# A DiT block with 32 experts on one core: front projections in three float32r passes, a shared stream ring, and the last two experts in column groups

## The chip, the core and the metric

The kernel runs on one core of one Trainium2 chip. The metric is device time in microseconds of one execution: the median of the runs. One more execution was recorded by the hardware profiler, and all rows below are from it. The engines are TensorE (PE in the rows, with its weight loads as PEld), VectorE (DVE), ScalarE (ACT), GpSimd (POOL) and SyncE (SP), whose queue issues the weight transfers.

## What is computed

One block of a diffusion transformer, in fp32, on 256 tokens of width 1024 with 256 context tokens: two kinds of attention with gates, then a mixture of 32 experts, four of them for each token.

```
h  = modulate(rms_norm(x), sh1, sc1);  hc = modulate(rms_norm(ctx), csh1, csc1)
p  = h @ w_in                            # keys, values, queries, two gates: 512 + 1024 + 2048 columns
k, v also from hc                        # context keys and values: the first 512 columns
y_a = global_attn(rope(norm(q_a)), k_a, v_a);  y_b = window_attn(rope(q_b), k_b, v_b, sink)
x  = x + g1 * ((sigmoid(g_a) * (y_a @ w_br_a) + sigmoid(g_b) * (y_b @ w_br_b)) @ w_o)
h2 = modulate(rms_norm(x), sh2, sc2)
combine = softmax of the 4 largest of (h2 @ w_router + b_router), else 0
for e in range(32):
    u   = h2 @ w_e1[e] + b_e1[e]
    act = min(u_glu, 7) * sigmoid(1.702 * u_glu) * (clip(u_lin, -7, 7) + 1)
    out = out + combine[:, e] * (act @ w_e2[e] + b_e2[e])
out = rms_norm(x + g2 * out, final_g)
```

The six shifts, scales and gates (`sh1` to `g2`) are a product of `w_mod` with the conditioning vector. The weights of the 32 experts are 12 MB each and by far the most of what is read.

## The kernel before

Every engine runs its instructions in the order in which the code issues them (a manual schedule), and semaphores hold an instruction until its operands are there.

**The stream.** All large weights come in one list, `pieces`, through SyncE's queue alone. `pump()` (line 100) issues the next pieces as long as there is room. Room is a ring of seven areas of 128 x 4096 words (2 MB, `N_PAIR`), each of two halves. An expert's piece takes a whole area: its first weights `w1` are four pieces, its second weights `w2` two. The pieces of the front (queries `q`, projections `in`, modulation `mod`, branches and `w_o`) take one half. `take` gives a piece to its user, `done` gives its room back. After attention two more areas join, `xx` (the tokens' and the context's transposes till then) and `ptt` (attention's probabilities till then). So nine areas serve the experts, and nothing else limits how far ahead the stream may run.

**The front.** Tokens and context lie in `xx` as `x` and `xc`, transposed. `m0_prod` (253) computes the part of the modulation that the projections need. `q_prods` (294) makes the 64 products of the queries, `gate_half` (393) the gates in sixteen groups of eight products, `proj` (383) the 32 products of the keys, `values` (467) the 32 of the values. Each is a 128 x 128 weight against 256 columns in fp32, and the profile shows each as two weight loads and two matmuls. `modulate_c` (302, 303) scales each of the eight rows of the context on VectorE and shifts it on ScalarE, both in place. `rotate` (375 to 378) applies the rotary embedding to a query or key in four VectorE steps. The rest of the modulation is a row times `w_mod`, in 32 steps of 128 x 1024: `mod_v` (351) on VectorE alone, or `mod_p` (357) on GpSimd with its sum on ScalarE, `mod_a` (364). Attention runs in steps of `scores` (517), `turn` (551) and `weigh` (567, 572), with the last gates and modulation steps between them. Then come the merge, `w_o` (723), the norm and the router.

**The experts.** For each pair of experts 64 slots each are gathered (830). `gemm1` (860) multiplies by `w1`, the activation is four steps (from 871), `act_turn` transposes its result, `gemm2` (897) multiplies by `w2`, and a product with the slots' matrix (918) adds the result to the tokens in `ACC`.

**The end.** The last two experts take another path. Their pieces are `l1` and `l2`: quarters and halves of columns, each in two transfers with short rows (line 130 for `w1`, line 124 for `w2`). `half1` (994) and `act_half` make the last expert's activation in two halves of columns, `half2` (1133) the second product in two halves, each followed by its scatter (1149, and 1017 for expert 30). In the middle stands a branch on the number of tokens that overflowed their expert's slots: every engine loads the count (1040) and compares (1041), and the code for overflowing tokens, which doesn't run with these inputs, lies behind it. The last lines scale by the final norm and store four blocks (1167).

## Time and profile before

| | us |
|---|---|
| median of 3 runs | 1210.23 (1209.86 to 1211.34) |
| profiled execution, its own time | 1209.79 |
| its span in the trace | 1208.0 |
| TensorE busy | 1147.9 (95% of the span) |
| VectorE, ScalarE, GpSimd busy | 360.0, 138.8, 35.1 |
| moved by DMA | 458.32 MB, mean 379 GB/s |

Busy time of TensorE is modelled, and a busy TensorE isn't one at its peak. In the rows a line such as `L393 PE MATMUL mm<-xx,ring 128*128 128x256 f32 x80` reads: line 393, engine, operation, written tile and read tiles (without buffer numbers), stationary and moving shape, and the number of records that are joined in it. What stands in brackets is the idle time of the engine before it and what ended that.

### The profile page before, as it was taken

What the parts mean: (1) busy time and instruction counts of PE and PEld (TensorE: products, weight loads), DVE (VectorE), ACT (ScalarE), POOL (GpSimd) and SP (SyncE); (2) the same over time, 40 slices, a digit from 0 to 9 for tenths busy, and PEclk for the clock granted to TensorE, in tenths of its full rate; (3) what the DMA queues carried; (4) which work ended last, traced back from release to release, by engine and by line L of the source; (5) the groups of instructions that cost most, each with busy time, mean ns of one, the idle gap of its engine ahead of it and who ended that gap; (6) DMA issues with size and microseconds to landing.
All of it is one profiled execution on the core that took longest, in us unless ns stands there. A gap on an engine that the chain in (4) does not pass through costs nothing. (4 is left out here: it accounts for less than half of the span.)

```text
span 1208.0 us, 13270 instructions
## 1 busy us (share of the span) xinstructions
PE 1147.9 (95%) x5624; PEld 531.5 (44%) x5624; DVE 360.0 (30%) x765; ACT 138.8 (11%) x304; POOL 35.1 (3%) x29
## 2 busy tenths in 40 slices
PE   7999999999999999999999999999999899999986
PEld 5888666883333424343434343333333232323221
DVE  3363665332122242223222221212222222222222
ACT  2122553021000000000000000000000000000002
POOL 0231100000000000000000000000000000000000
PEclk9999999999999999999999999999999999999998
DMA  9976641978999999999999999999999999999992
GB/s 379 385 301 213 240 175 53 352 296 335 427 428 428 427 427 428 427 427 428 427 429 427 428 428 425 430 427 427 429 426 426 428 428 428 429 426 429 417 396 89
DMA packets 43279, 458.32 MB, mean 379 GB/s; under 512 B 4872, under 2 KB 5264, under 8 KB 13776
## 3 DMA queue, kind: packets, MB, share of 16 engines
q1 hardware_dynamic: 41520, 454.05, 90.3%
q10 hardware_dynamic: 1296, 2.06, 0.5%
q0 software_dynamic: 400, 1.32, 0.3%
q8 instruction: 46, 0.75, 0.2%
q14 instruction: 17, 0.14, 0.0%
HBM read 456.36 MB, written 1.05 MB: 379 GB/s over the span
## 5 line engine op out<-in xcount | busy, mean ns | idle before, releaser
L860 PE MATMUL u<-ring,t 128*64 128x512 f32 x1472 | 337.3, 599 | 19.6 <-DMA ring<-w 19.2
L860 PEld LDWEIGHTS u<-ring,t 128*64 128x64 f32 x1472 | 100.7, 137 | 214.2 <-issue 178.2
L897 PE MATMUL y<-ring,r_q 128*64 128x512 f32 x832 | 183.8, 592 | 0.0
L908 DVE TENSOR_TENSOR t<-y,r_kv 64x512 f32<-64x512 f32 x60 | 41.3, 689 | 324.8 <-PE y L897 324.4
L897 PEld LDWEIGHTS y<-ring,r_q 128*64 128x64 f32 x832 | 59.7, 137 | 118.9 <-issue 116.3
L871 DVE TENSOR_SCALAR r_q<-u 128x512 f32<-128x512 f32 x31 | 21.4, 691 | 237.0 <-PE u L860 237.0
L860 PE MATMUL u<-ptt,t 128*64 128x512 f32 x336 | 78.2, 597 | 2.5 <-DMA ptt<-w 2.2
L873 ACT ACTIVATE r_q<-r_q 128x512 f32<-128x512 f32 x31 | 19.5, 630 | 499.1 <-DVE r_q L871 499.1
L713 PE MATMUL u<-mtx,keep 128*64 128x512 f32 x256 | 62.2, 605 | 3.0 <-DVE r_q L874 3.0
L830 PEld LDWEIGHTS xg<-mtx,r_y 128*128 128x128 f32 x512 | 58.4, 192 | 12.2 <-issue 12.2
L830 PE MATMUL xg<-mtx,r_y 128*128 128x128 f32 x512 | 61.3, 278 | 0.0
L393 PE MATMUL mm<-xx,ring 128*128 128x256 f32 x256 | 59.9, 385 | 0.0
L918 PE MATMUL sp<-t,mtx 128*128 128x512 f32 x120 | 59.5, 618 | 0.0
L393 PEld LDWEIGHTS mm<-xx,ring 128*128 128x128 f32 x256 | 47.3, 190 | 12.6 <-issue 5.0
L832 DVE TENSOR_TENSOR t<-xg,modb 128x512 f32<-128x512 f32 x32 | 22.1, 691 | 88.8 <-PE xg L830 88.8
L860 PEld LDWEIGHTS u<-ptt,t 128*64 128x64 f32 x336 | 23.2, 137 | 47.6 <-issue 40.7
L860 PE MATMUL u<-xx,t 128*64 128x512 f32 x176 | 39.8, 595 | 3.8 <-DMA xx<-w 3.8
L919 DVE TENSOR_TENSOR r_t<-r_t,sp 128x512 f32<-128x512 f32 x60 | 38.4, 680 | 5.1 <-PE sp L918 5.1
L918 PEld LDWEIGHTS sp<-t,mtx 128*128 128x128 f32 x120 | 20.3, 189 | 38.9 <-issue 38.9
L897 PE MATMUL y<-xx,r_q 128*64 128x512 f32 x160 | 36.0, 592 | 0.0
L713 PEld LDWEIGHTS u<-mtx,keep 128*64 128x64 f32 x256 | 16.3, 135 | 44.5 <-issue 22.6
L887 ACT COPY r_q<-ta 128x512 f32<-128x512 f32 x31 | 18.1, 585 | 145.4 <-PE ta L884 145.4
(247 smaller groups left out, 889.9 us busy)
## 6 DMA issues: line engine op xcount, KB each, us to landing
ring<-w SPq DMA_DIRECT2D x144, 2048.0 KB, 32.2
xx<-w SPq DMA_DIRECT2D x21, 2048.0 KB, 32.4
ptt<-w SPq DMA_DIRECT2D x21, 2048.0 KB, 29.7
ring<-w_mod SPq DMA_DIRECT2D x16, 1024.0 KB, 7.2
ring<-w_in SPq DMA_DIRECT2D x10, 1024.0 KB, 9.2
ring<-w_m SPq DMA_DIRECT2D x8, 1024.0 KB, 12.6
ring<-w SPq DMA_DIRECT2D x16, 512.0 KB, 17.8
ring<-w_q SPq DMA_DIRECT2D x8, 512.0 KB, 12.3
```

The costliest lines, as they stand in the source:

```text
L393: nc.tensor.matmul(gp[0][:, 0:256], w[:, k, :], x[:, k, :], start=(k == 0), stop=(k == 7))
L713: nc.tensor.matmul(u[c0:c0 + 64, ch % 2, :], ident[:, 4 * e + ch:4 * e + ch + 1].to_broadcast([128, 64]), be1, start=True, stop=False)
L830: nc.tensor.matmul(xp[:, b, :], z[:, tb, 128 * k:128 * k + 128], S[:, tb, :], start=(tb == 0), stop=(tb == 1))
L832: nc.vector.tensor_tensor(out=XT[p][:, 4 * h:4 * h + 4, :], in0=xp, in1=sh2[:, 4 * h:4 * h + 4].unsqueeze(2).to_broadcast([128, 4, 128]), ...
L860: nc.tensor.matmul(u[c0:c0 + 64, ch % 2, :], XT[p][:, k, 64 * j:64 * j + 64], w[:, 512 * ch:512 * ch + 512], start=False, stop=(k == 7))
L871: nc.vector.tensor_scalar(out=glu.rearrange("p (b f) -> p b f", b=2), in0=v[:, :, 0, :], scalar1=LIMIT, scalar2=None, op0=ALU.min)
L873: nc.scalar.activation(out=sg, in_=glu, func=AF.Sigmoid, scale=ALPHA)
L887: nc.scalar.copy(out=aT, in_=tp)
L897: nc.tensor.matmul(y[64 * h:64 * h + 64, :], l, w[:, 512 * h:512 * h + 512], start=(k == 0), stop=(k == 7))
L908: nc.vector.tensor_tensor(out=YY[p][64 * j:64 * j + 64, 512 * h:512 * h + 512], in0=y[64 * h:64 * h + 64, :], in1=g2[64 * h:64 * h + 64, 5 ...
L918: nc.tensor.matmul(sp, t[:, tb, :], y[:, s], start=True, stop=True)
L919: nc.vector.tensor_tensor(out=ACC[0][:, tb, s], in0=ACC[0][:, tb, s], in1=sp, op=ALU.add)
```

## The change

**Three passes.** A product in fp32 becomes three products of float32r operands. Each operand is split into a high part (a copy that rounds to float32r) and a low part (the operand less its high part): high by high, high by low, low by high (`mm3`). This holds for queries, keys, values and gates. `prep` splits a block of 1024 weight columns: ScalarE copies, VectorE (GpSimd for the four blocks of keys and values) subtracts, and with the second block the piece's half of the ring is given back. Five `part` buffers of 1 MB (2048 words) hold the parts, two of them the context's (`C3`). Tokens are split row by row into `X3`. Gates are prepared one group ahead, six of them within the attention loop.

**Room.** The ring has five areas instead of seven. The parts lie in a pool of the front, which is closed after attention, and four areas (`more0` to `more3`) are made in its place; with `xx` ten areas serve the experts. Attention's probabilities lie in `xx` and in `pt1`.

**The end.** The last expert's `w1` comes in whole rows as all others (three areas and two halves). The second weights of experts 30 and 31 are packed together by columns (`w2l`): three groups of 256 columns and two of 128. `last2` multiplies both experts' activations by one group, each in its half of TensorE's columns, and `scatter2` adds one group to the tokens, squares it and multiplies it by the final gain. The branch on overflow stands behind the stores.

Small ones: three small transfers go from GpSimd's queue to ScalarE's, one `mod_v` falls away from its place, a temporary of `settle` has moved.

```diff
-N_PAIR = 7
+N_PAIR = 5
...
-    halves1()
-    at = len(pieces) - 6
-    pieces[at:at] = [("w2", (NE - 2, k), w2[NE - 2, k]) for k in range(2)]
-    halves2()
+    w1s(NE - 1, range(3))
+    pieces.extend(("l1", k, w1[NE - 1, 3, :, 2048 * k:2048 * k + 2048]) for k in range(2))
+
+    pieces.extend(("w2", (NE, c), w2l[c]) for c in range(3))
+    pieces.extend(("l2", c, w2l[3, :, 2048 * c:2048 * c + 2048]) for c in range(2))
...
+    fz = fr.enter_context(tc.tile_pool(name="fz", bufs=1))
...
+    X3 = [fz.tile([128, 8, 256], F32R, name=n) for n in ("x_hi", "x_lo")]
...
+    def lower(lo, v, hi, eng=None):
+        (eng or nc.vector).tensor_tensor(out=lo, in0=v, in1=hi.bitcast(F32), op=ALU.subtract)
+
+    def part():
+        return fz.tile([128, 2048], F32R, name="part", tag="part", bufs=5)
+
+    def prep(kind, idx, b, eng=None):
+        w = take(kind, idx)[:, 1024 * b:1024 * b + 1024]
+        hl = part()
+        hi, lo = hl[:, 0:1024], hl[:, 1024:2048]
+        nc.scalar.copy(out=hi, in_=w)
+        lower(lo, w, hi, eng)
+        cut[kind, idx, b] = (hi, lo)
+        if b or kind == "q":
+            done(kind, idx)
...
+    def mm3(ps, lt, rt, start, stop, **kw):
+        nc.tensor.matmul(ps, lt[0], rt[0], start=start, stop=False, **kw)
+        nc.tensor.matmul(ps, lt[0], rt[1], start=False, stop=False, **kw)
+        nc.tensor.matmul(ps, lt[1], rt[0], start=False, stop=stop, **kw)
...
+        nc.scalar.copy(out=X3[0][:, j, :], in_=x[:, j, :])
+        lower(X3[1][:, j, :], x[:, j, :], X3[0][:, j, :])
...
             nc.vector.scalar_tensor_tensor(out=v, in0=v, scalar=a1[:, k, 1:2], in1=rinv_c, op0=ALU.mult, op1=ALU.mult)
-            nc.scalar.activation(out=v, in_=v, func=AF.Identity, bias=mod0[:, k, 0, 1:2])
+            nc.scalar.activation(out=C3[0][:, k, :], in_=v, func=AF.Identity, bias=mod0[:, k, 0, 1:2])
+            nc.vector.scalar_tensor_tensor(out=C3[1][:, k, :], in0=v, scalar=mod0[:, k, 0, 1:2], in1=C3[0][:, k, :].bitcast(F32),
+                                           op0=ALU.add, op1=ALU.subtract)
...
-            nc.tensor.matmul(gp[0][:, 0:256], w[:, k, :], x[:, k, :], start=(k == 0), stop=(k == 7))
+            mm3(gp[0][:, 0:256], [v[:, k, :] for v in w], [v[:, k, :] for v in X3], start=(k == 0), stop=(k == 7))
...
+    prep("in", 0, 0, nc.gpsimd)
...
+    prep("in", 0, 1, nc.gpsimd)
...
     modulate_c(range(8))
...
+    prep("in", 1, 0, nc.gpsimd)
+    prep("in", 1, 1, nc.gpsimd)
...
+            if qt == 1 and u < 6:
+                gate_prep(10 + u)
             mod_v()
...
+    fr.close()
+    lz = late.enter_context(tc.tile_pool(name="lz", bufs=1, reuse_waits="tile"))
+    for i in range(4):
+        grow(lz.tile([128, 4096], F32, name=f"more{i}"))
     grow(xx)
-    grow(ptt)
-    fr.close()
...
+    def last2(c):
+        n = groups[c][1]
+        w = (take("w2", (NE, c)) if c < 3 else take("l2", c - 3)).rearrange("p (e k c) -> p e k c", e=2, k=8)
+        wl[c] = ps2.tile([128, 512], F32, name="yl", tag=("y", "tp")[c % 2])
+        for k in range(8):
+            for j, aT in enumerate((aT0, aT1)):
+                nc.tensor.matmul(wl[c][64 * j:64 * j + 64, 0:n], aT[:, k % 4, 64 * (k // 4):64 * (k // 4) + 64],
+                                 w[:, j, k, :], start=(k == 0), stop=(k == 7))
...
+            a = ACC[0][:, tb, s]
+            sp = ps2.tile([128, 512], F32, name="sp", tag=("sp", "xg")[tb], bufs=2)
+            nc.tensor.matmul(sp[:, 0:n], TT[p][:, tb, :], y_t[0][:, 1, s], start=True, stop=True)
+            nc.vector.tensor_tensor(out=a, in0=a, in1=sp[:, 0:n], op=ALU.add)
+            nc.scalar.activation(out=x_t[:, tb, s], in_=a, func=AF.Square, accum_out=fin[:, tb, c:c + 1])
+            if c < 4:
+                nc.gpsimd.tensor_tensor(out=res[:, tb, s], in0=a, in1=fg[:, s], op=ALU.mult)
...
+    for c in range(5):
+        last2(c)
+        if c:
+            scatter2(c - 1)
+    scatter2(4)
```

VectorE where the context is modulated, before (`xx` holds the context, `a_150` the scales, `qa` a query's PSUM, `sh` and `r_q` the rotation's temporary and result):

```order
L235 RECIPROCAL rinv<-rinv 128x256
L302 SCALAR_TENSOR_TENSOR xx<-xx,a_150,rinv 128x256 x8
L375 STREAM_SHUFFLE sh<-qa 128x256
L376 TENSOR_TENSOR r_q<-qa,r_t 128x256
L377 TENSOR_TENSOR sh<-sh,r_t 128x256
L378 TENSOR_TENSOR r_q<-r_q,sh 128x256
```

VectorE's first rows at the same place after, with the line numbers of the changed kernel (`part` is a part of the context; the pair repeats up to eight times):

```order
L244 RECIPROCAL rinv<-rinv 128x256
L313 SCALAR_TENSOR_TENSOR xx<-xx,a_147,rinv 128x256
L315 SCALAR_TENSOR_TENSOR part<-xx,mod_146,part 128x256
L313 SCALAR_TENSOR_TENSOR xx<-xx,a_147,rinv 128x256
L315 SCALAR_TENSOR_TENSOR part<-xx,mod_146,part 128x256
L313 SCALAR_TENSOR_TENSOR xx<-xx,a_147,rinv 128x256
L315 SCALAR_TENSOR_TENSOR part<-xx,mod_146,part 128x256
L313 SCALAR_TENSOR_TENSOR xx<-xx,a_147,rinv 128x256
L315 SCALAR_TENSOR_TENSOR part<-xx,mod_146,part 128x256
L313 SCALAR_TENSOR_TENSOR xx<-xx,a_147,rinv 128x256
```

The eight scalings, which stood in a row ahead of the rotations, now have a subtraction behind each, and the rotations stand behind all sixteen.

SyncE's queue at the end of the front, before, from the last two pieces of `w_o` to the first areas of expert weights (`w` is an expert's weights; numbers are areas):

```order
L136 DMA ring_66<-w_o 128x2048 [waits DMAHW0_49,DVE_49,Activation_49]
L136 DMA ring_67<-w_o 128x2048 [waits DMAHW1_49,PE_49]
L136 DMA xx<-w 128x4096 [waits DMAHW2_49,PE_49,Activation_49]
L136 DMA ptt<-w 128x4096 [waits DVE_49,DMAHW3_49,PE_49,Activation_49]
L136 DMA ring_68<-w 128x4096 [waits DMAHW0_49,PE_49]
L136 DMA ring_62<-w 128x4096 [waits DMAHW4_49,DMAHW1_49,PE_49]
L136 DMA ring_65<-w 128x4096 [waits DMAHW5_49,DMAHW2_49,PE_49]
L136 DMA ring_63<-w 128x4096 [waits DMAHW6_49,DMAHW3_49,PE_49]
L136 DMA ring_64<-w 128x4096 [waits DMAHW7_49,DMAHW4_49,PE_49]
L136 DMA ring_66<-w 128x4096 [waits DMAHW5_49,PE_49]
```

The same place of SyncE's queue after, where `more` are the four new areas:

```order
L118 DMA ring_64<-w_o 128x2048 [waits DMAHW0_49,Activation_49]
L118 DMA ring_65<-w_o 128x2048 [waits DMAHW1_49,DVE_49]
L118 DMA more_1960<-w 128x4096 [waits DMAHW2_49,PE_49]
L118 DMA more_1962<-w 128x4096 [waits DMAHW7_49]
L118 DMA more_1964<-w 128x4096 [waits DMAHW0_49]
L118 DMA more_1966<-w 128x4096 [waits DVE_49,DMAHW2_49,PE_49,Activation_49]
L118 DMA xx<-w 128x4096 [waits DMAHW3_49]
L118 DMA ring_66<-w 128x4096 [waits DMAHW4_49,PE_49]
L118 DMA ring_63<-w 128x4096 [waits DMAHW5_49,DVE_49,PE_49]
L118 DMA ring_62<-w 128x4096 [waits DMAHW6_49,PE_49]
L118 DMA ring_64<-w 128x4096 [waits DMAHW7_49,PE_49]
L118 DMA ring_65<-w 128x4096 [waits DMAHW3_49,DMAHW1_49,PE_49]
```

The first expert pieces went to `xx`, `ptt` and then the ring; now they go to the four areas of the closed pool, to `xx` and then the five of the ring.

SyncE's queue at the end, before, from the last expert's first weights to the load of the overflow count:

```order
L130 DMA xx<-w 128x2x512 [waits DMAHW6_49,PE_49]
L130 DMA xx<-w 128x2x512 [waits DMAHW7_49,PE_49]
L124 DMA ptt<-w 128x2x512 [waits DMAHW0_49,PE_49]
L124 DMA ptt<-w 128x2x512 [waits DMAHW1_49,PE_49]
L124 DMA ptt<-w 128x2x512 [waits DMAHW2_49,PE_49]
L124 DMA ptt<-w 128x2x512 [waits DMAHW3_49,PE_49]
L124 DMA ring_68<-w 128x2x512 [waits DMAHW4_49,PE_49]
L124 DMA ring_68<-w 128x2x512 [waits DMAHW5_49,PE_49]
L124 DMA ring_68<-w 128x2x512 [waits DMAHW6_49,PE_49]
L124 DMA ring_68<-w 128x2x512 [waits DMAHW7_49,PE_49]
L1040 TENSOR_LOAD cint [waits DVE_49]
L1040 ISA x2
```

The same place of SyncE's queue after (`w2l` is the packed second weights, `more_1964` then holds the result):

```order
L118 DMA ring_62<-w 128x2048 [waits DMAHW5_49,PE_49]
L118 DMA ring_62<-w 128x2048 [waits DMAHW6_49,PE_49]
L118 DMA ring_64<-w2l 128x4096 [waits DMAHW7_49,PE_49]
L118 DMA ring_65<-w2l 128x4096 [waits DMAHW0_49,PE_49]
L118 DMA more_1960<-w2l 128x4096 [waits DMAHW1_49,PE_49]
L118 DMA more_1962<-w2l 128x2048 [waits DMAHW2_49,PE_49]
L118 DMA more_1962<-w2l 128x2048 [waits DMAHW3_49,PE_49]
L1078 DMA out<-more_1964 128x512 [waits DMAHW4_49,Activation_49]
L1078 DMA out<-more_1964 128x512 [waits DMAHW5_49,DVE_49,Pool_49]
L1078 DMA out<-more_1964 128x512 [waits DMAHW6_49,Activation_49]
L1078 DMA out<-more_1964 128x512 [waits DMAHW7_49,DVE_49,Pool_49]
L1082 TENSOR_LOAD cint [waits DVE_49]
```

Rows of 512 words in pairs have become rows of 2048 and 4096 words, and the stores stand ahead of the load of the count and its branch, on SyncE as on the other engines.

## Rows read from the trace of the kernel before

**Rows 1.** The page's slices: GB/s moved in each of 40 equal parts of the span.
```profile
GB/s 379 385 301 213 240 175 53 352 296 335 427 428 428 427 427 428 427 427 428 427 429 427 428 428 425 430 427 427 429 426 426 428 428 428 429 426 429 417 396 89
```

**Rows 2.** Busy by stretch: us, PE, PEld, DVE, ACT, POOL, PEclk, DMA share, GB/s.
```profile
130.00:140.00 10.00, 10.00 (x65) 6.82 (x66) 6.38 (x13) 5.47 (x13) 2.39 (x1) 1.00 0.60 204
270.00:300.00 30.00, 28.52 (x152) 12.46 (x152) 7.21 (x25) 5.10 (x11) 0.00 (x0) 1.00 0.80 327
800.00:1000.00 200.00, 187.44 (x888) 69.94 (x886) 43.99 (x82) 8.41 (x15) 0.00 (x0) 1.00 1.01 427
1180.00:1185.00 5.00, 5.00 (x12) 1.47 (x12) 0.00 (x0) 0.00 (x0) 0.00 (x0) 0.66 0.49 186
1185.00:1190.00 5.00, 4.40 (x19) 1.26 (x18) 1.60 (x4) 2.19 (x4) 0.00 (x0) 1.00 0.03 10
```

**Rows 3.** SyncE's issues in time: start us, us, queue, line, operation, tiles, count.
```profile
222.22 42.36 SPq L136 DMA_DIRECT2D ring<-w  x7
...
278.02 0.33 SPq L136 DMA_DIRECT2D xx<-w  x1
...
1170.65 5.15 SPq L124 DMA_DIRECT2D ring<-w  x4
...
1202.76 1.91 SPq L1167 DMA_DIRECT2D out<-r_t  x4
```

**Rows 4.** The groups by line: busy, mean ns of one, idle before and its end.
```profile
L860 PE MATMUL u<-ring,t 128*64 128x512 f32 x1472 | 337.3, 599 | 19.6 <-DMA ring<-w 19.2
...
L830 PEld LDWEIGHTS xg<-mtx,r_y 128*128 128x128 f32 x512 | 58.4, 192 | 12.2 <-issue 12.2
...
L830 PE MATMUL xg<-mtx,r_y 128*128 128x128 f32 x512 | 61.3, 278 | 0.0
...
L871 DVE TENSOR_SCALAR r_q<-u 128x512 f32<-128x512 f32 x31 | 21.4, 691 | 237.0 <-PE u L860 237.0
...
L873 ACT ACTIVATE r_q<-r_q 128x512 f32<-128x512 f32 x31 | 19.5, 630 | 499.1 <-DVE r_q L871 499.1
...
L351 DVE SCALAR_TENSOR_TENSOR ring<-ring,crow 128x1024 f32<-128x1024 f32 x22 | 26.2, 1210 | 0.0
```

**Rows 5.** TensorE in time: start us, us, engine, line, operation, tiles, count.
```profile
18.80 1.99 PE L294 MATMUL qa<-xx,ring 128*128 128x256 f32 x8
...
81.28 3.70 PE L467 MATMUL vp<-ring,xx 128*128 128x256 f32 x16
...
97.01 17.43 PE L393 MATMUL mm<-xx,ring 128*128 128x256 f32 x80
...
134.18 1.90 PE L572 MATMUL y<-ptt,r_kv 128*64 128x256 f32 x16
...
136.00 1.99 PE L393 MATMUL mm<-xx,ring 128*128 128x256 f32 x8
...
306.63 3.84 PE L830 MATMUL xg<-mtx,r_y 128*128 128x128 f32 x32
...
310.39 1.94 PE L860 MATMUL u<-ring,t 128*64 128x512 f32 x8
...
1179.90 3.10 PE L994 MATMUL u<-xx,t 128*64 128x512 f32 x8 [4.70 <-PEq L1041]
```

**Rows 6.** VectorE, ScalarE and GpSimd in time while the context is modulated (68 to 76 us).
```profile
68.30 3.26 DVE L302 SCALAR_TENSOR_TENSOR xx<-xx,a,rinv 128x256 f32<-128x256 f32 x8
...
68.82 3.30 ACT L303 ACTIVATE xx<-xx,mod 128x256 f32<-128x256 f32 x8 [2.95 <-DVE xx L302]
...
71.81 2.35 POOL L357 TENSOR_TENSOR ring<-ring,crow 128x1024 f32<-128x1024 f32 x1 [5.94 <-DMA ring<-w_mod]
...
72.15 2.29 DVE L377 TENSOR_TENSOR sh<-sh,r_t 128x256 f32<-128x256 f32 x1
...
75.50 0.42 DVE L377 TENSOR_TENSOR sh<-sh,r_t 128x256 f32<-128x256 f32 x1
```

**Rows 7.** Instructions of line 1041: durations in ns (min/median/max), first and last start.
```profile
L1041 PEldq COMPARE_BRANCH  x1: 6172/6172/6172, 1173.6 to 1173.6; - x1
```

More of the change, by code (lines that the diff above doesn't have):

```diff
@@ L291, in q_prods @@
     def q_prods(j, cs):
-        w = take("q", j)
+        w = cut["q", j, 0]
         for c in cs:
-            nc.tensor.matmul(qa[c // 4][:, c % 4, :], w[:, 128 * c:128 * c + 128], x[:, j, :],
-                             start=(j == 0 and c % 2 == 0), stop=(j == 7), skip_group_check=True)
+            mm3(qa[c // 4][:, c % 4, :], [v[:, 128 * c:128 * c + 128] for v in w], [v[:, j, :] for v in X3],
+                start=(j == 0 and c % 2 == 0), stop=(j == 7), skip_group_check=True)
     hc_pend = []
@@ L380, in proj @@
     def proj(ps, i, b, src, stop=True):
-        w = take("in", i)[:, 1024 * b:1024 * b + 1024].rearrange("p (k c) -> p k c", k=8)
+        w = parts_of("in", i, b)
         for k in range(8):
-            nc.tensor.matmul(ps, w[:, k, :], src[:, k, :], start=(k == 0), stop=(k == 7))
+            mm3(ps, [v[:, k, :] for v in w], [v[:, k, :] for v in src], start=(k == 0), stop=(k == 7))
     gp = [None]
@@ L430, in tile_dit_block @@
     nc.scalar.dma_start(out=tmk, in_=consts[:, C_TRI:C_END])
+    C3.extend(part().rearrange("p (k c) -> p k c", k=8) for _ in range(2))
     modulate_c(range(8))
@@ L856, in gemm1 @@
         for k in ks:
-            w = take("w1", (e, k // 2))[:, 2048 * (k % 2):2048 * (k % 2) + 2048]
+            if e == NE - 1 and k > 5:
+                w = take("l1", k - 6)
+            else:
+                w = take("w1", (e, k // 2))[:, 2048 * (k % 2):2048 * (k % 2) + 2048]
             for ch in (0, 2, 1, 3):
@@ L919, in scatter @@
                 nc.vector.tensor_tensor(out=ACC[0][:, tb, s], in0=ACC[0][:, tb, s], in1=sp, op=ALU.add)
-    def scatter_one(e, tb):
-        for h in range(2):
-            s = slice(512 * h, 512 * h + 512)
-            sp = ps2.tile([128, 512], F32, name="sp", tag=("sp", "xg")[tb], bufs=2)
-            nc.tensor.matmul(sp, TT[e][64 * h:64 * h + 64, tb, :], YY[e][64 * h:64 * h + 64, :],
-                             start=True, stop=True)
-            nc.vector.tensor_tensor(out=ACC[0][:, tb, s], in0=ACC[0][:, tb, s], in1=sp, op=ALU.add)
     def settle():
@@ new lines, in tile_dit_block @@
+    scatter(p - 1, (0,))
+    u = bias1(e1)
+    gemm1(e1, u, (0,))
+    aT0 = act_turn(e0)
+    gemm1(e1, u, range(1, 8))
+    act(e1, u)
+    scatter(p - 1, (1,))
+    nc.scalar.activation(out=junk, in_=eps, func=AF.Sqrt)
+    aT1 = act_turn(e1, tmp4[:, 1, :].rearrange("p (b s) -> p b s", b=4))
+    fin = moe.tile([128, 2, 8], F32, name="fin")
+    res = areas[spare[0][0]].rearrange("p (a c) -> p a c", a=4)[:, 0:2, :]
+    spare.pop(0)
+    groups = [(0, 256), (256, 256), (512, 256), (768, 128), (896, 128)]
@@ new lines, in tile_dit_block @@
+    wl = {}
+    def last2(c):
[6 more added lines that the diff above has]
+                                 w[:, j, k, :], start=(k == 0), stop=(k == 7))
+        o = groups[c][0]
+        s = slice(o, o + n)
+        nc.vector.tensor_tensor(out=y_t[0][:, 1, s], in0=wl[c][:, 0:n], in1=g2[:, s], op=ALU.mult)
@@ new lines, in scatter2 @@
+    def scatter2(c):
+        o, n = groups[c]
+        s = slice(o, o + n)
+        for tb in range(2):
+            a = ACC[0][:, tb, s]
[5 more added lines that the diff above has]
+                nc.gpsimd.tensor_tensor(out=res[:, tb, s], in0=a, in1=fg[:, s], op=ALU.mult)
+            if c == 3:
+                nc.vector.reduce_sum(fin[:, tb, 5:6], fin[:, tb, 0:4], axis=AX.X)
+                nc.vector.tensor_scalar(out=fin[:, tb, 5:6], in0=fin[:, tb, 5:6], scalar1=1.0 / 1024, scalar2=EPS,
+                                        op0=ALU.mult, op1=ALU.add)
+            elif c == 4:
+                nc.scalar.activation(out=fin[:, tb, 6:7], in_=fin[:, tb, 4:5], func=AF.Sqrt, bias=fin[:, tb, 5:6],
+                                     scale=1.0 / 1024)
@@ L1116, in tile_dit_block @@
             body(e)
-    half1(1, 2, u)
-    scatter_e0(1)
-    half1(1, 3, u)
-    act_half(1, u)
-    nc.scalar.activation(out=junk, in_=eps, func=AF.Sqrt)
-    fin = moe.tile([128, 2, 4], F32, name="fin")
-    aT = tmp4[:, 3, :].rearrange("p (b s) -> p b s", b=4)
-    yl = [ps2.tile([128, 512], F32, name="yl", tag="y")]
-    def half2(h, q):
-        w = take("l2", 2 * h + q).rearrange("p (k c) -> p k c", k=4)
-        for b in range(4):
-            k = 2 * q + 4 * (b // 2) + b % 2
-            nc.tensor.matmul(yl[h][64 * (k % 2):64 * (k % 2) + 64, :], aT[:, k % 4, 64 * (k // 4):64 * (k // 4) + 64],
-                             w[:, b, :], start=(q == 0 and b < 2), stop=(q == 1 and b >= 2))
```

197 lines of the change are left out of this document (71 added, 126 removed).

## The prediction

> **What bounds the kernel now.** I read the profile in this order: the slices of the page, the busy table by stretch, SyncE's issues, the groups by line, then the timelines of the stages that the change touches.
>
> From the eleventh slice to the thirty-seventh the DMA engines move 425 to 430 GB/s [rows 1]; in 800 to 1000 us their share is 1.01 at 427 GB/s [rows 2]. TensorE is busy too, but there only for 187.44 of 200 us [rows 2], and the first matmuls of an expert wait 19.2 us in all for the ring [rows 4]. So the experts run at the pace of the weight stream, and that pace can't rise. The end is fixed by when the stream stops having gaps, how many bytes are left then, and what follows the last byte.
>
> The gaps lie in the front. Areas to load into come free only as TensorE uses them up: in 270 to 300 us the stream makes 327 GB/s [rows 2], since the seven ring areas had been asked for by 264.6 us and the tenth area only at 278.02, when expert 0 had used the first [rows 3]. I call that moment T1. At T1 all nine areas are full.
>
> The stream's end is not clean either. SyncE issues the last four short transfers from 1170.65 to 1175.8 us [rows 3]; in 1180 to 1185 us 186 GB/s flow, in 1185 to 1190 us 10 GB/s, or 50 KB [rows 2], so the last byte lands near 1185.3. From there to the end of the span are 22.7 us.
>
> **The stream's end.** The last three slices carry 417, 396 and 89 GB/s over 30.2 us each [rows 1]: 27.2 MB, of which 1.05 MB are the output, so 26.2 MB of weights after 1117.4 us. At 427.5 GB/s that takes 61.3 us and ends at 1178.7. The change loads the last two experts in long rows like all others (8 and 16 KB for each partition instead of 2 KB), so I take that rate to the end: **-6.6 us**. Bounds: 0 (the short pieces were not the cause) and -6.6.
>
> **The ring.** At T1 before, 9 areas of 2.097 MB are full; after it 10 (five ring areas, four of the freed front room, xx). One area less remains to be loaded: 2.097 / 427.5 = **-4.9 us**. It needs all ten full at T1: the last ring area is asked for when the last w_o piece is used, 13.4 us before T1 as now (264.6 to 278.02), and one area takes 4.9 us. In the front itself the smaller ring (10 halves for 14) costs nothing that I can find: halves with projection weights are now freed by the copy that splits them, before TensorE uses them.
>
> **The front.** What counts is T1. Of 256 fp32 products (128 gates, 64 queries, 32 keys, 32 values) each becomes three. Now one takes 17.3/40 = 0.432 us (40 in a run, 80 records [rows 5]: each is two loads and two matmuls). The trace holds no product in three exact parts. From below, a quarter of 0.432, 0.108 us a pass, which is one column in each cycle of the granted 2.4 GHz. From above, a pass bound by the 0.192 us that a weight load of 128 columns takes [rows 4]. The nearest row is the gather, where one load of 128 columns comes to each short matmul: 61.3/512 = 0.120 by its busy time [rows 4], 3.76/32 = 0.1175 from start to start [rows 5]. I take 0.1175, so 0.3525 for a product, 0.08 less than now, 20.4 us over all 256.
>
> By the Trainium skill (FP8 and Floating Point Precision, TensorE Precision Notes) true FP32 is four passes and the reduced form reads the word and truncates it; no run here shows the reduced form. At a quarter, 0.108 us, the 144 products of values and late gates would take another 4 us off, and the time would be 1188.
>
> Little of the 20.4 us survives, since VectorE and ScalarE now make the parts:
>
> *Queries.* The first product starts at 18.80 us [rows 5]. Now it waits for two steps on x for each of two rows (some 0.8 us in series each) and for the subtraction on the first q block, 1024 elements at 1.2 us (the price of L351 [rows 4]), behind the remaining scalings of x: about 23.3. Each of the 64 products gains 0.08, or 5.1, so the queries end about where they did.
>
> *Context.* Now eight VectorE steps take 3.26 us, ScalarE's eight follow at the same pace, 68.30 to 72.1 [rows 6]. After, VectorE alternates: scale, wait for ScalarE's part, subtract, scale. One round is a scaling of 0.41 (3.26/8), ScalarE's part of 0.41 (3.30/8), a subtraction at the 0.42 of a rotation step that runs alone (75.50), and two hand-overs of 0.11 (68.82 - 68.30 - 0.41): 1.46 [rows 6]; eight are 11.7 us, **8.4 more**. I let the chain start 2.3 earlier, near 66.0: the sixteen gates ahead of it save 1.3, and I count a blocked rotation of some 1 us fewer there. It ends near 77.7. TensorE has only some products of the keys meanwhile, then stands. The four rotations of queries behind the chain take 1.48 each (72.15 to 75.50, less the block told below [rows 6]) and hold the PSUM that the values need.
>
> *GpSimd.* A VectorE step on two SBUF operands that takes 0.42 us alone (75.50) took 2.29 beside a GpSimd step of 2.35 (72.15), so it was blocked for 1.87 [rows 6]. After the chain GpSimd has two subtractions and some four products of the mod weights back to back, where now these stand 5 us and more apart. I count two such steps of 2.35 whole, 4.7 us, on the rotations: values start at 77.7 + 5.9 + 4.7 = 88.3 for 81.28 now [rows 5], **+7.0 us**. Bounds: no block (+2.3) and all six (+16.4).
>
> *Values and the fourteen remaining gates.* 144 products at -0.08: **-11.4 us**.
>
> *Attention.* Half of these gates stand between the steps of attention, where VectorE is busy 6.38 of 10 us already [rows 2]; six subtractions of 1.2 us come in. Of the 4.5 us that the seven gates save there I give back **+2.5** (bounds 0 and 4.5). TensorE comes out of its long waits at a lower clock: after the 4.7 us wait at 1175 us eight matmuls took 3.10 us [rows 5] for 1.94, at a granted clock of 0.66 in that stretch [rows 2], and I add **+1.5** (0 to 3).
>
> Sum of the front: 7.0 - 11.4 + 2.5 + 1.5 = **-0.4 us**, with ends at -9 and +12.5. Rows from the merge to expert 0 are the same instructions as now.
>
> **After the last byte.** Name that moment D. The last piece of expert 31's first weights lands 8.39 MB earlier, D - 19.6. Then four matmuls (1.8), the activation 0.69 + 0.63 + 0.69 + 0.69, the copy that follows the transposes at ScalarE's 0.63 [rows 4], the transposes at some 0.5, with hand-overs: the first column group starts at D - 13.4. A pair of 256-column matmuls in the two column halves costs 1.82/4 = 0.455 us (from 134.18 to 136.00, sixteen records for four such pairs [rows 5]), so a group of 256 takes 3.64; of 128, half of that and a little, 1.96. Three and two of them, with three scatters of 0.9 between and 0.3 of waiting, end at D + 4.4. The last scatter then runs through VectorE's adds, ScalarE's squares with their sums, the root and the scaling, nine short steps in line of 0.3 to 0.65 us: the first store is issued at D + 10.2, the four issues take 1.9, and from there to the end are 3.3 us now (1202.76 + 1.91 to 1208.0 [rows 3]): D + 15.4. The branch on the overflow count, which held TensorE for 6.17 us in the middle of the last expert [rows 7], now stands behind the stores; TensorE can take it while the result is scaled, and I add 1.0 (0 to 6). Together 16.4 for 22.7: **-6.3 us**.
>
> **Sum.** 1208.0 - 6.6 - 4.9 - 0.4 - 6.3 = 1189.8 of span. The profiled execution is 1.8 us longer than its span, 1209.79, and lies 0.4 under the median 1210.23. So 1191.6, with the median's offset **1192 us**.
>
> **Rivals.**
> *A. The front keeps its gain* (-9, at the bound): VectorE's blocks by GpSimd don't come together and attention hides the subtractions. 1183. For it: GpSimd's steps are paced by the arrival of the mod weights today. Against: after the chain those weights have long landed.
> *B. Every GpSimd step blocks a VectorE step.* All six in a row: 9.4 us more, 1201. For it: both cases in the rows ended with GpSimd's step. Against: a block costs only what is left of GpSimd's step. By the Trainium skill (SBUF — State Buffer, Who interferes with whom) a VectorE step with two SBUF inputs and a GpSimd step that reads SBUF exclude each other, and the second to start waits for the whole of the first. The trace agrees (2.29 for 0.42 us).
> *C. Slower: a pass costs its weight load.* If the load of 0.192 us isn't hidden, each of the 672 passes outside the keys (whose 96 lie in the wait anyway) costs 0.0745 more: 50.1 us, 1242. It decides from 0.1175 + 18.2/672 = 0.145 us a pass: above it the kernel is slower than now. Against: it is the gather's own load, and there it still fits under 0.1175.
> *D. The end doesn't follow.* The stream keeps its slow end, or the branch behind the stores is waited for in full: 6.6 or 5 us more, 1197 to 1204.
> *E. TensorE becomes the bound.* Its slack against the stream is some 25 us of waiting (19.2 of it in one row [rows 4]); one more area uses 4.9. If it were gone, only front and end would count, 1204.
>
> **How the numbers follow.** Forecast with B and D's milder ends (1184 to 1200): 0.70. A: 0.10. B full or D full (1200 to 1206): 0.09. E: 0.03. C and anything else past 1212: 0.08. The range 1180 to 1205 leaves out C and the far ends. A measurement of this kernel tells 0.2%, 2.4 us, from no change. Faster by more: 0.88; within: 0.04 (the edge between B, E and C); slower: 0.08.
>
> **What would show it.** Right: a DMA row at 427 GB/s up to the last slice; ten 2 MB issues before the stream runs without gaps; VectorE alternating with ScalarE for 11 to 12 us near 66 to 78 us with TensorE mostly idle; passes of 0.11 to 0.12 us; from the last landing to the end 15 to 17 us. Wrong: T1 far from 278 us, passes over 0.145 us, or gaps in the stream after T1, any of which moves the time by its own length.

## The result: slower by 1.7%, all of it in the front

The changed kernel takes 1231.32 us (1230.19 to 1233.01, 4 runs), the kernel before 1210.13 in the same session: a ratio of 1.0174, 95% interval 1.0157 to 1.0192. The forecast was 1192 us.

The split of the difference needs three moments of the trace. T1 is the issue of the first area that expert 0 gives back. SyncE's issues after, with the columns of [rows 3]:

```profile
313.77 11.15 SPq L118 DMA_DIRECT2D more<-w  x4
...
1222.91 2.87 SPq L1078 DMA_DIRECT2D out<-more  x4
```

T1 is 313.77 us, for 278.02 before: **35.75 us later**. The slices show it as well (the columns of [rows 1]): the steady rate begins in the twelfth slice instead of the eleventh, and the ten slices ahead hold 2398 instead of 2729 GB/s in sum.

```profile
GB/s 378 368 179 61 261 142 162 287 352 208 355 428 428 427 426 429 428 428 426 428 427 430 427 426 427 430 426 426 430 427 428 428 428 429 428 428 426 427 428 189
```

The last byte lands near 1212.5 us (the stretches of the end, columns of [rows 2]: 106 KB flow in 1212 to 1214, at the rate before it 0.5 us):

```profile
1210.00:1212.00 2.00, 2.00 (x22) 1.41 (x17) 0.00 (x0) 0.00 (x0) 0.09 (x1) 1.00 0.53 221
1212.00:1214.00 2.00, 2.00 (x20) 1.48 (x20) 1.27 (x3) 0.67 (x3) 0.62 (x1) 1.00 0.14 53
```

| | before | after | moved | forecast |
|---|---|---|---|---|
| start to T1 | 278.0 | 313.8 | +35.75 | -0.4 |
| T1 to the last byte | 907.3 | 898.7 | -8.6 | -11.5 |
| last byte to the end of the span | 22.7 | 16.9 | -5.8 | -6.3 |
| span | 1208.0 | 1229.4 | +21.4 | -18.2 |

So the end of the change gives 14.4 of the 17.8 us that were forecast for it, and the front takes this back two and a half times.

**Where the front loses.** The product in exact parts has the price that was taken. TensorE's rows of one query step, ten passes from 32.37 to 33.56:

```profile
24.54 0.41 PE L213 MATMUL qa<-x_hi,part 128*128 128x256 f32 x1
...
26.24 0.41 PE L215 MATMUL qa<-x_hi,part 128*128 128x256 f32 x1
...
32.37 0.28 PE L214 MATMUL qa<-x_lo,part 128*128 128x256 f32 x1
...
33.56 0.28 PE L215 MATMUL qa<-x_hi,part 128*128 128x256 f32 x1
```

That is 0.119 us a pass (0.1175 was taken). In the first step, behind waits of 2.8 and 0.9 us, eight passes from 24.54 to 26.24 took 0.2125 us each. The granted clock was 0.50 from 24.5 to 26.5 us, the lower of its two levels, and 0.67 in the mean of this stretch (columns of [rows 2]):

```profile
25.00:30.00 5.00, 5.00 (x40) 4.55 (x39) 1.47 (x5) 0.41 (x1) 0.00 (x0) 0.67 1.03 421
```

The context's chain takes what was forecast too, but starts later, and what stands behind it is far slower. VectorE after, with start, duration, line and tiles (L313 scales, L315 subtracts; L395 and L396 are those two of a rotation's four steps that have both operands in SBUF):

```profile
72.35 0.48 DVE L313 SCALAR_TENSOR_TENSOR xx<-xx,a,rinv 128x256 f32<-128x256 f32 x1
73.41 0.48 DVE L315 SCALAR_TENSOR_TENSOR part<-xx,mod,part 128x256 fp32r<-128x256 f32 x1 [0.58 <-ACT part L314]
73.81 0.48 DVE L313 SCALAR_TENSOR_TENSOR xx<-xx,a,rinv 128x256 f32<-128x256 f32 x1
...
84.68 2.54 DVE L395 TENSOR_TENSOR sh<-sh,r_t 128x256 f32<-128x256 f32 x1
87.26 2.48 DVE L396 TENSOR_TENSOR r_q<-r_q,sh 128x256 f32<-128x256 f32 x1
...
90.34 1.93 DVE L395 TENSOR_TENSOR sh<-sh,r_t 128x256 f32<-128x256 f32 x1
92.30 2.44 DVE L396 TENSOR_TENSOR r_q<-r_q,sh 128x256 f32<-128x256 f32 x1
```

GpSimd at the same time (two subtractions of L194, five products of L375):

```profile
84.59 4.87 POOL L194 TENSOR_TENSOR part<-ring,part 128x1024 fp32r<-128x1024 f32 x2 [14.68 <-ACT part L203]
89.42 12.51 POOL L375 TENSOR_TENSOR ring<-ring,crow 128x1024 f32<-128x1024 f32 x5
```

And the first product of the values on TensorE, which waits for the last rotation:

```profile
100.44 0.58 PE L213 MATMUL vp<-part,x_hi 128*128 128x256 f32 x1 [8.53 <-DVE r_q L394]
```

One turn of the chain takes 73.81 - 72.35 = 1.46 us, eight 11.7. The rotations behind it take 18.6 us (84.02 to 102.58) instead of 5.9: of their steps with two operands in SBUF, seven take 1.9 to 2.5 us instead of 0.42. From 84.59 to 101.9 us GpSimd works without a break. The values start at 100.44 instead of 81.28 us [rows 5].

The largest loss is in attention, which runs in eight rounds. Each begins with a product (L599, before L567), and in six of the eight this product waits for VectorE. The starts of two rounds after:

```profile
196.00 0.66 PE L599 MATMUL y<-keep,st 128*64 128x128 f32 x8 [0.26 <-DVE r_y L609]
...
208.57 0.66 PE L599 MATMUL y<-keep,st 128*64 128x128 f32 x8 [1.77 <-DVE r_y L609]
```

and two before, which had been in the trace all along:

```profile
166.54 0.66 PE L567 MATMUL y<-keep,st 128*64 128x128 f32 x8 [0.22 <-DVE r_y L577]
...
177.34 0.66 PE L567 MATMUL y<-keep,st 128*64 128x128 f32 x8 [0.41 <-DVE r_y L577]
```

A round takes 12.57 instead of 10.80 us. VectorE at the start of such a round, after (a reciprocal, the split, a modulation step) and before (the reciprocal and the modulation step):

```profile
196.04 0.17 DVE L577 RECIPROCAL st<-st 128x2 f32<-128x2 f32 x1
196.74 1.23 DVE L194 TENSOR_TENSOR part<-ring,part 128x1024 fp32r<-128x1024 f32 x1 [0.53 <-ACT part L203]
197.88 1.22 DVE L369 SCALAR_TENSOR_TENSOR ring<-ring,crow 128x1024 f32<-128x1024 f32 x1
```

```profile
166.59 0.17 DVE L545 RECIPROCAL st<-st 128x2 f32<-128x2 f32 x1
166.67 1.20 DVE L351 SCALAR_TENSOR_TENSOR ring<-ring,crow 128x1024 f32<-128x1024 f32 x1
```

The split costs a wait of 0.53 us for ScalarE's copy and 1.14 us of its own. The modulation step starts 1.84 us behind the reciprocal instead of 0.08, and the 1.76 us between them are what the round has grown. VectorE waits for no transfer in these rounds.

The first two rounds are longer still, 15.40 and 14.48 us (they start at 153.54 and 168.94, the third at 183.42) instead of 11.65 and 10.59. In them and ahead of them four VectorE steps stand beside GpSimd's last five products: a split of 2.74 us for 1.23, two modulation steps of 3.38 and 3.42 for 1.20 and a step of 2.08 for 0.16, 7.8 us more together. These products run between 129.63 and 180.88 us, since three of them wait for their weights; before, the last four ran between 109.30 and 132.80. From the first scores to the merge's first `w_o` product 139.0 us pass (129.6 to 268.6) instead of 118.1 (114.4 to 232.5): 20.9 us of the 35.75.

### The profile page after: what moved, and what is told of

It is laid out like the page before. It is cut to its first block, busy times and chain, and to the rows that moved or that the text cites. A ratio compares the mean times of both kernels' runs of the same rounds, so it can differ in the third digit from the quotient of the medians.

```text
span 1229.4 us, 14045 instructions
## 1 busy us (share of the span) xinstructions
PE 1145.0 (93%) x5978; PEld 547.4 (45%) x5978; DVE 411.3 (33%) x807; ACT 169.5 (14%) x349; POOL 49.3 (4%) x35
## 3 DMA queue, kind: packets, MB, share of 16 engines
q10 hardware_dynamic: 1744, 3.38, 0.7%
## 4 chain that ended last, share of the span: by engine, by line
PE 51%; DMA 35%; DVE 8%; ACT 4%; issue 1%; ACTq 0%; SPq 0%; DVEq 0%
PE u L899 20%; DMA ring<-w 19%; DMA more<-w 16%; PE y L938 8%; PE xg L866 3%; PE u L749 3%; PE o L759 2%; PE sp L955 2%; PE br L629 2%; ACT xx L567 2%; DVE ring L369 1%; DVE st L557 1%; PE yl L1039 1%; DVE part L194 1%; PE ta L925 1%
## 5 line engine op out<-in xcount | busy, mean ns | idle before, releaser
L899 PE MATMUL u<-ring,t 128*64 128x512 f32 x1008 | 230.5, 599 | 11.4 <-DMA ring<-w 11.2
L899 PE MATMUL u<-more,t 128*64 128x512 f32 x832 | 190.8, 599 | 8.0 <-DMA more<-w 7.7
L899 PEld LDWEIGHTS u<-ring,t 128*64 128x64 f32 x1008 | 70.1, 137 | 149.5 <-issue 127.2
L899 PEld LDWEIGHTS u<-more,t 128*64 128x64 f32 x832 | 57.3, 137 | 119.7 <-issue 102.8
L938 PE MATMUL y<-ring,r_q 128*64 128x512 f32 x480 | 106.1, 592 | 0.0
L938 PE MATMUL y<-more,r_q 128*64 128x512 f32 x384 | 85.5, 592 | 0.0
L938 PEld LDWEIGHTS y<-ring,r_q 128*64 128x64 f32 x480 | 34.5, 137 | 68.5 <-issue 67.4
L938 PEld LDWEIGHTS y<-more,r_q 128*64 128x64 f32 x384 | 27.6, 137 | 54.8 <-issue 54.2
L213 PE MATMUL mm<-x_hi,part 128*128 128x256 f32 x128 | 39.2, 306 | 0.0
L194 DVE TENSOR_TENSOR part<-ring,part 128x1024 fp32r<-128x1024 f32 x24 | 31.0, 1297 | 20.9 <-ACT part L203 20.9
```

The costliest lines, as they stand in the source:

```text
L194: (eng or nc.vector).tensor_tensor(out=lo, in0=v, in1=hi.bitcast(F32), op=ALU.subtract)
L213: nc.tensor.matmul(ps, lt[0], rt[0], start=start, stop=False, **kw)
L899: nc.tensor.matmul(u[c0:c0 + 64, ch % 2, :], XT[p][:, k, 64 * j:64 * j + 64], w[:, 512 * ch:512 * ch + 512], start=False, stop=(k == 7))
L938: nc.tensor.matmul(y[64 * h:64 * h + 64, :], l, w[:, 512 * h:512 * h + 512], start=(k == 0), stop=(k == 7))
```

## The experiments

The theory after the result had three causes, one behind the other on the way to T1: GpSimd's steps in a row (about 12 us), the chain's turns (4.4), the splits in attention (16). Rivals were the ring of five areas, through which the modulation weights come late (the stream moves 61, 142 and 162 GB/s in the fourth, sixth and seventh slices), and TensorE's own passes and clock. T1 is compared, since it leaves the end out. The six edits of the changed kernel ran once each, beside the kernel before at 1212.65 us (the first four) and 1212.81 us (the last two); the edits of the kernel before ran four or five times. T1 can differ by 3 us between executions with the same front (see the end alone below), so a smaller gain shows nothing by itself.

**No GpSimd products.** Left out are the ten products of modulation weights on GpSimd.

```diff
     def mod_p():
         t, w = mod_start()
-        nc.gpsimd.tensor_tensor(out=w, in0=w, in1=crow, op=ALU.mult)
         mod_sum.append((t, w))
```

> The changed kernel without GpSimd's ten products of the modulation weights (ScalarE sums the weights as they are, so the later shifts, scales and gates are other numbers; everything else runs as before). Theory: GpSimd's steps stand in a row beside the rotations behind the context's chain and block them for 12.7 us, and a few more block VectorE in attention; five of the seven in the row fall away, so the values start near 92 instead of 100.4, T1 comes 10 to 14 us earlier than 313.8, and the time is near 1219. Rival (VectorE's long steps are due to something else, or the modulation weights come late through the smaller ring anyway): values within 1 us of 100.4 and 1231 us.

VectorE in that kernel:

```profile
84.85 2.55 DVE L394 TENSOR_TENSOR sh<-sh,r_t 128x256 f32<-128x256 f32 x1
...
87.44 2.48 DVE L395 TENSOR_TENSOR r_q<-r_q,sh 128x256 f32<-128x256 f32 x1
...
90.51 0.41 DVE L394 TENSOR_TENSOR sh<-sh,r_t 128x256 f32<-128x256 f32 x1
```

T1, on SyncE:

```profile
299.08 11.15 SPq L118 DMA_DIRECT2D more<-w  x4
```

Two steps are blocked, by the two subtractions that are left; the next ones take 0.41 and 0.43. Values start at 93.6 and T1 is 14.7 us earlier, 1217.95 us. The theory holds, and the rival that VectorE is slow for another reason falls. But only 6.9 of the 14.7 us lie ahead of the values. The other 7.8 lie in attention, where the four long steps are gone too.

**The chain in three rows.** The loop over the eight rows of the context is cut in three.

```diff
             nc.vector.scalar_tensor_tensor(out=v, in0=v, scalar=a1[:, k, 1:2], in1=rinv_c, ...)
+        for k in ks:
+            v = xc[:, k, :]
             nc.scalar.activation(out=C3[0][:, k, :], in_=v, func=AF.Identity, ...)
+        for k in ks:
+            v = xc[:, k, :]
             nc.vector.scalar_tensor_tensor(out=C3[1][:, k, :], in0=v, ...)
```

> The changed kernel with the context's chain in three rows: all eight scalings, then ScalarE's eight parts, then the eight subtractions; same work. Theory (VectorE's turns with ScalarE cost 11.7 us where the work itself needs 3.3 + 0.5 + 3.3): the chain takes 7 to 7.5 us, the values start some 4.4 earlier (96), T1 follows, 1227 us. Rival (the rotations behind the chain wait for GpSimd's row of steps anyway, which ends when it ends): values as before at 100.4, 1231 us.

```profile
72.53 3.26 DVE L313 SCALAR_TENSOR_TENSOR xx<-xx,a,rinv 128x256 f32<-128x256 f32 x8
75.71 3.25 DVE L319 SCALAR_TENSOR_TENSOR part<-xx,mod,part 128x256 fp32r<-128x256 f32 x8
```

```profile
309.20 11.15 SPq L118 DMA_DIRECT2D more<-w  x4
```

These are VectorE's rows and T1. The chain takes 6.4 us instead of 11.7, the values start at 94.7, T1 comes 4.6 us earlier, 1226.93 us. Nothing is left out here, so this is a repair that the changed kernel could have had.

**No late splits.** The last six gates' weights are not split; these gates use the parts of the gate before.

```diff
     def gate_prep(m):
-        if m < 16:
+        if m > 9:
+            cut["in", 2 + m // 2, m % 2] = cut["in", 6, 1]
+            if m % 2:
+                done("in", 2 + m // 2)
+        elif m < 16:
             prep("in", 2 + m // 2, m % 2)
```

> The changed kernel without the splits of the last six gates' weights, which stand within attention (these gates use the parts of the gate before, so the work of TensorE is the same and the gates' values are others). Theory (VectorE's and ScalarE's chain sets attention's pace, 12.6 us a round instead of 10.7 with 1.2 + 1.05 us of splitting in it): the rounds take 10.7 us again, attention 100 to 103 instead of 117.8 us, T1 14 to 18 us earlier, near 1215 us. Rival (attention is slow because modulation weights come late through five areas, or because of TensorE's clock of 0.91 there): rounds above 12 us, 1226 us or more.

Two rounds on TensorE, and T1:

```profile
188.17 0.66 PE L603 MATMUL y<-keep,st 128*64 128x128 f32 x8 [0.80 <-DVE r_y L613]
...
198.98 0.66 PE L603 MATMUL y<-keep,st 128*64 128x128 f32 x8 [1.00 <-DVE r_y L613]
```

```profile
300.97 11.15 SPq L118 DMA_DIRECT2D more<-w  x4
```

The rounds are back at 10.81 us, with the passes and the modulation steps as they were and nearly the same granted clock (0.93 from 140 to 240 us, 0.90 in the changed kernel). So VectorE's row of steps sets them, and neither the passes nor the clock does. The edit also gives the gates' room back earlier, but late weights can't have set the rounds of 12.57 us, since VectorE waited for no transfer in them. From the first scores to `w_o` pass 125.0 us (130.8 to 255.8) instead of 139.0. T1 gains 12.8 us, a little less than the 14 to 18 expected, since attention began 1.2 us later; the time is 1219.45 us.

**All three.** The three edits together.

> The three edits together: no GpSimd products, the chain in three rows, no late splits (outputs are other numbers as in the single ones). Theory (the three causes lie behind each other on the path to T1): the gains add, T1 near 313.8 - 12 - 4.4 - 16 = 281 us and the time near 1199. Rival (one cause hides behind another): less than the sum, 1207 us or more.

```profile
283.46 11.15 SPq L118 DMA_DIRECT2D more<-w  x4
```

T1 gains 30.3 us where the single edits gain 14.7, 4.6 and 12.8, 32.1 in all: they lie behind each other with little overlap. The splits are worth 14.0 us of attention's time (139.0 to 125.0), GpSimd's products 8.0 (139.0 to 131.0 without them). The time is 1202.04 us. Of the 5.4 us by which T1 is still later than before, 4.7 are there when the chain starts (73.0 for 68.3 us).

**The values' splits on VectorE.** Does the order of GpSimd's queue make the row? In it the modulation products stand behind the subtractions for the values, and these wait for copies that ScalarE makes after the chain.

```diff
-    prep("in", 1, 0, nc.gpsimd)
-    prep("in", 1, 1, nc.gpsimd)
+    prep("in", 1, 0)
+    prep("in", 1, 1)
```

> The changed kernel with the two subtractions for the values' weights on VectorE instead of GpSimd. In the changed kernel GpSimd's modulation products stand behind these two, which wait for ScalarE's copies behind the context's chain, and so all seven run together beside the rotations. Theory (the order of GpSimd's queue gathers the steps there, and a VectorE step with two operands in SBUF is blocked wherever it meets one): GpSimd's five products run from about 71 to 83 us, beside the chain; the chain's steps are blocked in turn, by 5 x 1.9 us, so it ends near 93, the rotations take 5.9 us again, and the values start near 101: no gain, 1230 us. Rival (the chain's steps aren't blocked, only rotations are): chain as before to 84, values at 92.5, T1 8 us earlier, 1223 us.

GpSimd, VectorE's chain, and T1:

```profile
70.58 10.12 POOL L375 TENSOR_TENSOR ring<-ring,crow 128x1024 f32<-128x1024 f32 x4
```

```profile
76.59 1.91 DVE L315 SCALAR_TENSOR_TENSOR part<-xx,mod,part 128x256 fp32r<-128x256 f32 x1 [0.57 <-ACT part L314]
78.43 2.56 DVE L313 SCALAR_TENSOR_TENSOR xx<-xx,a,rinv 128x256 f32<-128x256 f32 x1
81.56 0.48 DVE L315 SCALAR_TENSOR_TENSOR part<-xx,mod,part 128x256 fp32r<-128x256 f32 x1 [0.57 <-ACT part L314]
```

```profile
310.92 11.15 SPq L118 DMA_DIRECT2D more<-w  x4
```

Four products now run from 70.58 us on, since nothing holds them in the queue, and the chain is hit instead: scalings and subtractions take 1.91 and 2.56 us until GpSimd is done, 0.48 after. The chain ends at 90.7, the rotations take 5.9 us again, the values start at 99.0, T1 gains 2.9 us, and the time is 1229.20 us. So the gathering comes from the queue's order, the block isn't a matter of rotations, and moving the row elsewhere beside a busy VectorE gains nothing that one run could show.

**One pass.** Left out are two of the three passes of every product, so the products are coarser.

```diff
-        nc.tensor.matmul(ps, lt[0], rt[0], start=start, stop=False, **kw)
-        nc.tensor.matmul(ps, lt[0], rt[1], start=False, stop=False, **kw)
-        nc.tensor.matmul(ps, lt[1], rt[0], start=False, stop=stop, **kw)
+        nc.tensor.matmul(ps, lt[0], rt[0], start=start, stop=stop, **kw)
```

> The changed kernel with the first of the three passes alone (high by high; the low parts are made but not used, so the products are coarser). Theory (the front waits for VectorE, ScalarE and GpSimd from the chain to the end of attention; TensorE sets the pace of the queries alone, at 24 passes of 0.119 us a step): queries up to 7 us shorter, where the stream of 1.5 MB a step (3.6 us) then limits, values and the first gates some 10 us shorter as far as VectorE's splits allow, attention's rounds as they were at 12.6 us: T1 8 to 15 us earlier, 1216 to 1223. Rival (passes and the clock of TensorE make the loss): T1 25 us earlier or more, 1206 or less.

```profile
183.51 0.66 PE L597 MATMUL y<-keep,st 128*64 128x128 f32 x8 [1.76 <-DVE r_y L607]
...
196.09 0.66 PE L597 MATMUL y<-keep,st 128*64 128x128 f32 x8 [1.77 <-DVE r_y L607]
```

```profile
301.91 11.15 SPq L118 DMA_DIRECT2D more<-w  x4
```

Attention's rounds stay at 12.58 us with a third of the gates' passes. Taking away two thirds of all passes moves T1 by 11.9 us, a third of the loss, and 1220.18 us is still 7 more than the kernel before took beside it. So TensorE's passes explain a third of the loss at most.

**The ring of five, in the kernel before.**

```diff
-    spare = [(i, h) for i in range(N_PAIR) for h in range(2)]
+    spare = [(i, h) for i in range(N_PAIR - 2) for h in range(2)]
...
     grow(ptt)
+    spare.extend((i, h) for i in (N_PAIR - 2, N_PAIR - 1) for h in range(2))
+    pump()
```

> The kernel before with five of its seven ring areas in the front; the other two join behind attention with the last two, so that nine serve the experts as before. Theory (the forecast's: the smaller ring costs the front nothing, the front is set by the order of VectorE's steps): T1 within 1 us of 278.0 and 1210 us. Rival (modulation weights come too late through a ring of five, and the gap in the stream at 90 to 120 us of the changed kernel is the cause of the loss): T1 later by 10 us or more, 1220 us and above.

Attention's first rounds, and T1:

```profile
134.01 0.66 PE L567 MATMUL y<-keep,st 128*64 128x128 f32 x8
...
146.93 1.12 PE L567 MATMUL y<-keep,st 128*64 128x128 f32 x8 [2.82 <-DVE r_y L577]
...
158.75 0.66 PE L567 MATMUL y<-keep,st 128*64 128x128 f32 x8
```

```profile
283.90 0.33 SPq L136 DMA_DIRECT2D xx<-w  x1
```

The ratio is 1.0034 (1.0010 to 1.0059), 4 us; in the profiled execution T1 comes 5.9 us later. The front is as before up to attention, whose first two rounds take 12.92 and 11.82 us instead of 11.65 and 10.59. The last pair of modulation weights is issued at 148 to 157 us instead of 125 to 132. Another 3 us come between the first `w_o` product and T1 (48.6 for 45.5). So the small ring does cost something in this kernel, 4 to 6 us against a loss of 35.75 in T1. What it costs in the changed kernel, by the late weights of GpSimd's last products, no run tells apart. Both sides expected something else: it was told to be free, the rival wanted 10 us.

**The end alone**, with the front, the ring and the nine areas of before; then **with an eighth ring area**, so ten for the experts. The edits are the end's part of the diff above, and

```diff
-N_PAIR = 7
+N_PAIR = 8
```

> The kernel before with the new end alone (whole rows, column groups of the last two experts' second weights, the branch behind the stores, the three small transfers on ScalarE's queue); front, ring of seven and nine areas as before. Theory (the end as a whole is worth what it gave in the changed kernel): T1 stays at 278.0; from T1 to the last byte 898.5 + 4.9 = 903.4 us instead of 907.3, and 17.1 us behind it instead of 22.7: span 1198.5, 1200 us. Rival (the short rows were not what thinned the stream): last byte at 1185.3, 1204 us. Rival (the forecast's full rate to the end): last byte at 1178.7, 1197.5 us.

> The same with a ring of eight areas instead of seven, so ten areas for the experts, as in the changed kernel, but with the fp32 front of before. Theory (one area more is worth its transfer, 4.9 us): 1195 us. Rival (the tenth area isn't full at T1, or the front is what limits): as the kernel with nine areas, 1200 us.

T1, the start's clock and the last bytes of the first of them:

```profile
280.98 0.33 SPq L118 DMA_DIRECT2D xx<-w  x1
```

```profile
20.00:25.00 5.00, 5.00 (x29) 3.68 (x22) 2.42 (x8) 0.37 (x1) 0.00 (x0) 0.75 1.01 410
1184.00:1186.00 2.00, 2.00 (x19) 1.28 (x17) 1.27 (x3) 0.47 (x3) 0.43 (x1) 1.00 0.16 61
```

It takes 1202.00 us, a ratio of 0.9921 (0.9900 to 0.9941). T1 is 3 us later with the same front. 1.3 us of that are there at 16.78 us, and 2.9 at 23.90 us (20.99 before), in a stretch with a granted clock of 0.75 where the kernel before had 1.00. From T1 to the last byte (1184.5) pass 903.5 us and 17.5 behind it, as the theory said (903.4 and 17.1).

With ten areas 1197.17 us, 0.9878 (0.9856 to 0.9900). The area is worth 4.8 us; a transfer is 4.9. This kernel is faster than both the one before and the changed one. Its stream's end:

```profile
1165.00:1170.00 5.00, 3.81 (x30) 2.39 (x32) 2.11 (x4) 1.58 (x3) 0.00 (x0) 1.00 0.98 413
1170.00:1175.00 5.00, 5.00 (x43) 3.51 (x40) 0.85 (x2) 0.00 (x0) 0.00 (x0) 1.00 0.87 365
1175.00:1180.00 5.00, 5.00 (x39) 3.50 (x37) 1.35 (x4) 0.94 (x4) 1.42 (x2) 1.00 0.49 205
```

Even with long rows the last 5 MB flow at falling rates, so short rows were only part of it. What the new end mended are the two slices ahead of the last: 427 and 428 GB/s in the changed kernel for 417 and 396 [rows 1], some 3 us of the stream by an estimate from these four figures. From 1166.1 to 1186.3 us TensorE is busy without a break and waits for no transfer. Why the rate falls at the end no run tells.

## Why the prediction was wrong, step by step

**What bounds the kernel** held: the stream runs at 425 to 430 GB/s from T1 nearly to its end in every kernel, and T1, the number of areas and the end add up.

**The ring**, -4.9: right (4.8 between the two kernels of the end). That it costs the front nothing was wrong by 4 to 6 us in the kernel before.

**The stream's end**, -6.6: 3.7 came (898.7 + 4.9 for 907.3). The full rate to the last byte, which the forecast took, did not come.

**After the last byte**, -6.3: 5.8 came, by the steps that were forecast: the first store is issued 10.4 us behind the last byte (1222.91), 10.2 were forecast.

**The front**, -0.4, ends -9 and +12.5: +35.75. By its steps:

| step | forecast | measured | off |
|---|---|---|---|
| first pass of the queries | 23.3 | 22.5, waits to 24.2 | about 0 |
| start of the context's chain | 66.0 | 72.35 | +6.3 |
| chain | 11.7 | 11.7 | 0 |
| chain to the values (rotations and blocks) | 10.6 | 16.4 | +5.8 |
| values to the first scores | 26.1 | 29.2 | +3.1 |
| first scores to `w_o` | 117.6 | 139.0 | +21.4 |

The steps that failed:

*Attention*, the largest. "Of the 4.5 us that the seven gates save there I give back +2.5 (bounds 0 and 4.5)": the bound took for granted that TensorE sets the pace there, so that splitting can at worst eat what the passes save. The row read for it, VectorE busy 6.38 of 10 us [rows 2], is a share. Much of VectorE's idle time was its waits for ScalarE (13.6 us in all of attention for the exponentials, 13.4 for the copy behind each round's products), within one row of steps that already set the rounds at 10.8 us: they keep 10.81 us without the late splits, although each gate then takes eight products of 0.357 us instead of 0.432. The trace of before says so in TensorE's waits (waiting and releasing line, total us, times, longest), in each of six rounds:

```profile
PE y L567 <- DVE r_y L577: 4.6, 6, 1.7
```

After, the same wait:

```profile
PE y L599 <- DVE r_y L609: 12.6, 6, 3.8
```

A split put into that row lengthens it in full, 1.76 us a round. Without the late splits attention is 14.0 us shorter. The other part is GpSimd's: its five late products, which the prediction did not look for in attention, are worth 8.0 us there; singly the two gains are a little more than the 20.9 us lost. What the +1.5 for TensorE's clock stands for was not told apart.

*GpSimd.* "I count two such steps of 2.35 whole": the mechanism, VectorE's steps blocked for the whole of GpSimd's, was right, and so was the row (six steps back to back were forecast, seven came). Its size was wrong: six steps ahead of the values were blocked, not two, 11.2 us beyond their 0.42 each. A rotation has two steps with both operands in SBUF, and as long as the row lasts each of them meets a new step of GpSimd. The row comes about since the change puts subtractions that wait for ScalarE ahead of products that before ran one by one from 50.75 us on. The Trainium skill (SBUF — State Buffer, Who interferes with whom) says that a VectorE step with two inputs in SBUF and a GpSimd step that reads SBUF exclude each other; the trace agrees with it in seven steps out of seven, at 1.9 to 2.5 us for 0.42. Without GpSimd's products the values start 6.9 us earlier.

*Start of the chain.* The saving in the passes was counted ahead of it (1.3 for sixteen gates, a block fewer), yet the queries begin 3.7 us later and do not make it up: their first step takes 7.77 us (22.50 to 30.27) where the next take 4.50, with the waits and the low clock shown above, and the first gate starts at 58.95 instead of 55.20. Behind that GpSimd's two subtractions for the keys block two rotations there (1.76 and 1.75 us for 0.42; before, one step took 1.58). What each part of this is worth was not tried apart, so the cause of these 6.3 us stays open in part.

*Values to scores.* Of the 7 us that 88 products should give, 3.9 came. Only 72 of them stand in this stretch, worth 5.8 us at 0.08, and behind the wait of 8.53 us the first fourteen passes took 0.2125 us each, 1.3 us more in all (from 100 to 105 us the granted clock was 0.66).

Of the rivals, B was right for the row ahead of the values (six blocks, 14.1 us by its price, 11.2 measured) and had nothing for the larger loss behind it. C, the slower one, got the sign right by a mechanism that wasn't there (a pass of 0.119, not 0.145 or more); that is luck. A slower attention paced by VectorE was not among them, and the range had no room for it.
